# Down projection: weight sums in their own tile, made one item early; sevens and eights alternate; bank sums added by DMA

## The chip, the cores and the metric

The kernel runs on one core of a Trainium2 chip. A core has five engines, each with its own instruction queue that is worked through in order: TensorE (PE, matrix products), VectorE (DVE), ScalarE (ACT), GpSimd (POOL) and SyncE (SP, which here issues the loads of the weights). They meet only through semaphores. The metric is the time of one execution on the device in microseconds (us), as a median of runs. PE ran at its upper clock level, 2.4 GHz, all along: the granted clock of the profiled run is 0.996.

## What is computed

One layer on 256 tokens of width 2048. The change concerns its last sub-layer, a dense squared-ReLU MLP with a hidden width of 8192, and there the second product:

```python
x = x + rmsnorm(merged @ w_out[l], post_mix_g[l])
h = rmsnorm(x, pre_mlp_g[l])
f = jnp.square(jax.nn.relu(h @ w_up[l])) @ w_down[l]
x = x + rmsnorm(f, post_mlp_g[l])
```

Before it stands a token mixing part with four branches under sigmoid gates; one of its stages, the gate logits, uses the same product scheme as the down projection.

## The kernel before

**Weights.** Every product is made in three: weights and activations are split into a high and a low part, and PE computes high x high, high x low and low x high (L808 to L810 in `eight_sums`). The weights come in *items* of 1 MB, listed in program order by `w_items`. `w_emit` takes the next item, lets SP load it into one of three `raw` buffers, and cuts it into *pieces* of up to 128 x 1024. Of each piece `split` (L101 to L103) makes `hi` (ACT, a cast, L102) and `lo` (DVE, a subtraction, L103); both have four buffers. `w_get` keeps four pieces emitted ahead of the one PE works on. So a cast waits until PE is done with the piece four back, a load until the last reader of the item three back is done.

**Sums of weights.** The down projection works in groups. In a group `eight_sums` runs over eight items p, each with two weight blocks of 128 x 1024, and accumulates in eight PSUM banks (M1 to M8, four of tag `bank`, four of tag `aux`). An *eight* item is two pieces with four products each (24 matmuls). A *seven* item uses sums and differences of weight blocks and of activations (`sx`) and needs seven products instead of eight (21 matmuls) in four pieces: the first half of the item, a quarter of it, and two pieces of sums. The function `seven` makes these sums on DVE in the item's own `raw` buffer, the first behind the first piece's split (L161, 128 x 1024), the others behind the second's (L164, L165, 128 x 512):

```python
def first():
    V.tensor_tensor(b4[:, :, 0], b4[:, 1], b4[:, :, 0], ALU.subtract)
def second():
    V.tensor_tensor(b4[:, 1, 1], b4[:, 1, 1], b4[:, 0, 0], ALU.subtract)
    V.tensor_tensor(b4[:, 0, 1], b4[:, 0, 1], b4[:, 1, 1], ALU.subtract)
return [(b4[:, 0], first), (b4[:, 1, 1], second), (b4[:, :, 0], None), (b4[:, :, 1], None)]
```

`SEVEN` lists which p are sevens in the down stage, (1, 2, 4, 5); `SEVEN_G` does so for the gate stage, (1, 3, 5), where the same scheme runs six times.

**Stages.** The hidden width is worked in four quarters q. Each quarter has an up stage (`up`, blocks of 128 hidden columns, which also makes `sx` by `keep_sums`) and then two down groups h = 0, 1 one directly behind the other; the last quarter has one group, and then a plain product (`dn`) for the other half. `evac` (L1161 to L1166) moves a finished bank into `acc[h]`: in q = 0 by a copy on ACT (L1164), later by an add on DVE (L1166). `eight_sums` calls it one piece after the bank's last product (`late`, `settle`). `combine` (L1113) then adds the eight sums on DVE. The order on each engine is set by a scheduler from the program's dependencies; the rows of the change below show it.

Of the kernel before, what the change touches and what calls it, by code (L numbers as in the profile page):

```python
# [8 lines left out]
F32 = mybir.dt.float32  # L9
# [3 lines left out]
ALU = mybir.AluOpType  # L13
AX = mybir.AxisListType

P = 128
# [10 lines left out]
PC = 2048  # L27
CONSTS = P + 32 + 6 * 4 + 4 * CW
HC = 1024
# [3 lines left out]
QK_SCALE = 192 ** -0.5  # L33
TWO_PI = 6.283185307179586

SEVEN = (1, 2, 4, 5)
SEVEN_G = (1, 3, 5)


# [35 lines left out]
def trunk(ctx: ExitStack, tc: tile.TileContext, t: dict):  # L75
    nc = tc.nc
    V, A, G, T = nc.vector, nc.scalar, nc.gpsimd, nc.tensor

    cst = ctx.enter_context(tc.tile_pool(name="cst", bufs=1))
    wp = ctx.enter_context(tc.tile_pool(name="wp", bufs=1))  # L80
# [11 lines left out]
    def w2(name):  # L92
        return sm.tile([P, 512], F32, tag="w2", name=name, bufs=5)
# [56 lines left out]
    items = w_items()  # L150
    ready = []
    pending = []
    newest = []

    def seven(raw):


        b4 = raw.rearrange("p (a b n) -> p a b n", a=2, b=2)

        def first():  # L160
            V.tensor_tensor(b4[:, :, 0], b4[:, 1], b4[:, :, 0], ALU.subtract)  # L161

        def second():
            V.tensor_tensor(b4[:, 1, 1], b4[:, 1, 1], b4[:, 0, 0], ALU.subtract)  # L164
            V.tensor_tensor(b4[:, 0, 1], b4[:, 0, 1], b4[:, 1, 1], ALU.subtract)  # L165
        return [(b4[:, 0], first), (b4[:, 1, 1], second), (b4[:, :, 0], None), (b4[:, :, 1], None)]

    def w_emit():
        if not pending:
            it = next(items, None)  # L170
            if it is None:
                return False
            src, n, step = it
            raw = wp.tile([P, PC], F32, tag="raw", name="raw", bufs=3)
            if isinstance(step, str):
                nc.sync.dma_start(raw.rearrange("p (c n) -> p c n", c=2), src)
                pending.extend(seven(raw) if step == "seven" else [(raw[:, :HC], None), (raw[:, HC:], None)])
            else:
                nc.sync.dma_start(raw[:, :n], src)
                pending.extend((raw[:, o:min(n, o + step)], None) for o in range(0, n, step))  # L180
        src, then = pending.pop(0)
        hi = wp.tile([P, HC], F32R, tag="hi", name="hi", bufs=4)
        lo = wp.tile([P, HC], F32R, tag="lo", name="lo", bufs=4)
        if len(src.shape) == 3:
            parts = [a.rearrange("p (a n) -> p a n", a=2) for a in (hi, lo)]
        else:
            parts = [a[:, :src.shape[1]] for a in (hi, lo)]
        newest[:] = [e.ins for e in split(src, *parts)]
        if then:
            then()  # L190
        ready.append((hi, lo))
        return True

# [107 lines left out]
    for k in range(0, KD, 2):  # L301
        nc.sync.dma_start(xT[:, k:k + 2], t["xT"][:, k:k + 2])
        w = None
        for j in range(k, k + 2):
            if k < 4 or w is None:
                w, o = w_get(0), 0
# [237 lines left out]
    for b in range(4):  # L544
        ps = [bank("cva"), bank("cvg")]
# [174 lines left out]
    for b in range(4):  # L720
        ps = bank("su")
        block_tr(ps, hx)
        c = su[:, b * S:(b + 1) * S]
# [146 lines left out]
    for j in range(4):  # L870
        acc = None
        gts = [None] * 4
        for n, (xs, need, nk) in enumerate(order):
# [9 lines left out]
            elif n % 2 == 0:  # L883
                assert not tasks.live

                first = n + (n == 0)
# [26 lines left out]
            if n == 0:  # L913
                if j:
                    until(lambda: f"mx{j - 1}" in done)
                acc = t4n("acc")
# [44 lines left out]
    for c in range(4):  # L961
        ps = [bank(f"o{i}") for i in range(NT)]
        for k in range(0, KD if c < 3 else 8, 2):
            if c == 0 and k == 12:
# [3 lines left out]
                mp = ctx.enter_context(tc.tile_pool(name="mp", bufs=1))  # L968
# [109 lines left out]
    def keep_sums(p, ue, uo):  # L1078
        i = SEVEN.index(p)
        split(sums(ue, uo), sx[:, i, 0], sx[:, i, 1])  # L1080

    def first_hidden(fx):
# [17 lines left out]
            yield 1  # L1100
        done.add("u0")

    dr = ctx.enter_context(tc.tile_pool(name="dr", bufs=1, space=bass.MemoryType.DRAM))
    kept = dr.tile([P, NT, D], F32, name="kept")
    xr = mp.tile([P, NT, D], F32, tag="og", name="xr")
# [2 lines left out]
    acc = [None, None]  # L1108
# [29 lines left out]
    for q in range(NQ):  # L1138
        fx = big.tile([P, KQ, 2, S], F32R, tag="B", name="fx")
        if q == 0:  # L1140
            spawn(first_hidden(fx))
            spawn(second_norm())
        if q == NQ - 1:
            spawn(combine(1, lambda *a: None))
        ue = None
        for b in range(4 if q == 0 else 0, KQ):
            ps = bank("up")
            block_tr(ps, h2)
            u = w1("u")
            join(u, ps)  # L1150
            V.scalar_tensor_tensor(u, u, 0.0, u, ALU.max, ALU.mult)
            split(u, fx[:, b, 0], fx[:, b, 1])
            if b // 2 in SEVEN:
                if b % 2:
                    keep_sums(b // 2, ue, u)
                ue = u
        until(lambda: {"u0", "r2"} <= done)
        if q == 0:
            acc[0] = mp.tile([P, 8, 512], F32, tag="oo", name="acc0")
            acc[1] = mp.tile([P, 8, 512], F32, tag="og", name="acc1")  # L1160

        def evac(h, b, ps):
            if q == 0:
                A.copy(acc[h][:, b], ps[b])  # L1164
            else:
                V.tensor_tensor(acc[h][:, b], ps[b], acc[h][:, b], ALU.add)  # L1166

        for h in range(2 if q < NQ - 1 else 1):
            eight_sums(fx, lambda i, o: tuple(sx[:, i, a, o * P:(o + 1) * P] for a in range(2)), SEVEN,
                       lambda b, ps, h=h: evac(h, b, ps))  # L1170
        settle()
# [17 lines left out]
    ps = [bank(f"dn{i}") for i in range(NT)]  # L1189
# [8 lines left out]
    ps = [bank(f"dn{i}") for i in range(NT)]  # L1198
# [107 lines left out]
```

## Time and profile before

| | us |
|---|---|
| median of 3 runs (1500.91 to 1505.73) | 1502.41 |
| the profiled execution | 1501.62 |
| its span | 1499.9 |
| PE busy in it | 1472.8 |
| DVE busy | 1205.1 |
| ACT busy | 800.8 |
| POOL busy | 20.0 |

PE is busy 98% of the span, DVE 80%, ACT 53%, the DMA engines some 55%. A matmul's busy time in the trace is its whole way through the array, 0.39 us for 512 columns, while the next one starts after 0.227 us; a stretch is therefore read by its length and its count of matmuls. Idle time of PE is named with the event that ended it.

### The profile page before, as it was taken

Reading aid. Unit: us, or ns where it says so; the run is one execution under the profiler, and the core shown is the slowest. Engines: PE = TensorE matmul, PEld = TensorE weight load, DVE = VectorE, ACT = ScalarE, POOL = GpSimd, SP = SyncE. Lnnn points to the kernel's source line nnn. Section 1 sums busy time; section 2 is a strip of 40 time slices with the busy share of each in tenths; the row PEclk is TensorE's granted clock in tenths of the full one; section 3 lists DMA queues with packets and bytes.
Section 4 is the critical chain, followed back from the end, with each engine's and each line's share of the span. In section 5 each row is a group of like instructions: output and inputs, shape, how many; then the busy total and the mean of one; then the engine's idle time right before and its main releaser. Section 6 shows DMA issues by size and latency. Waiting matters only on the chain.

```text
span 1499.9 us, 18735 instructions
## 1 busy us (share of the span) xinstructions
PE 1472.8 (98%) x7192; PEld 1236.3 (82%) x7192; DVE 1205.1 (80%) x1697; ACT 800.8 (53%) x1078; POOL 20.0 (1%) x36
## 2 busy tenths in 40 slices
PE   9999999999999999999999999999999999999997
PEld 7988888888888888888878887888778887788875
DVE  6878788977798798796668888777997779987886
ACT  6655655445555555554445656655554545555552
POOL 0100000000000000000000000000000000000000
PEclk9999999999999999999999999999999999999999
DMA  8655544544655655656656645655556545655563
GB/s 268 219 192 173 180 171 153 187 172 167 226 200 172 226 203 170 226 203 241 245 213 253 216 164 200 213 194 194 169 171 227 194 166 199 210 184 196 168 253 113
DMA packets 57113, 295.76 MB, mean 197 GB/s; under 512 B 5120, under 2 KB 5248, under 8 KB 36544
## 3 DMA queue, kind: packets, MB, share of 16 engines
q1 hardware_dynamic: 55072, 280.68, 53.7%
q0 software_dynamic: 1952, 13.89, 2.6%
q8 instruction: 56, 0.92, 0.2%
q14 instruction: 33, 0.27, 0.1%
HBM read 290.36 MB, written 4.19 MB: 196 GB/s over the span
## 4 chain that ended last, share of the span: by engine, by line
PE 90%; DVE 5%; ACT 2%; issue 1%; DMA 1%; POOL 0%; POOLq 0%; ACTq 0%; SPq 0%; DVEq 0%
PE up L216 15%; PE sum L810 10%; PE sum L809 10%; PE sum L808 10%; PE up L219 8%; PE yb L205 2%; PE yb L206 2%; PE yb L207 2%; ACT hi L102 2%; DVE lo L103 2%; PE zg L205 2%; PE zg L207 2%; PE zg L206 2%; PE o L206 2%; PE o L205 2%; PE o L207 2%
## 5 line engine op out<-in xcount | busy, mean ns | idle before, releaser
L102 ACT CAST hi<-raw 128x1024 fp32r<-128x1024 f32 (+3 forms) x624 | 621.3, 1012 | 461.0 <-PE sum L810 112.3
L103 DVE TENSOR_TENSOR lo<-raw,hi 128x1024 fp32r<-128x1024 f32 (+3 forms) x624 | 720.9, 1173 | 168.3 <-ACT hi L102 160.8
L216 PE MATMUL up<-h,hi 128*128 128x512 f32 x960 | 229.9, 391 | 0.0
L216 PEld LDWEIGHTS up<-h,hi 128*128 128x128 f32 x960 | 176.3, 188 | 34.1
L808 PE MATMUL sum<-hi,fx 128*128 128x512 f32 x308 | 121.6, 395 | 12.3 <-ACT hi L102 12.3
L219 PEld LDWEIGHTS up<-h,lo 128*128 128x128 f32 x960 | 123.1, 191 | 4.7
L219 PE MATMUL up<-h,lo 128*128 128x256 f32 x960 | 124.8, 283 | 0.0
L809 PE MATMUL sum<-lo,hx 128*128 128x512 f32 x312 | 121.4, 389 | 0.0
L810 PE MATMUL sum<-hi,hx 128*128 128x512 f32 x312 | 121.4, 389 | 0.0
L808 PE MATMUL sum<-hi,hx 128*128 128x512 f32 x312 | 121.4, 389 | 0.0
L809 PE MATMUL sum<-lo,fx 128*128 128x512 f32 x308 | 120.0, 390 | 0.0
L810 PE MATMUL sum<-hi,fx 128*128 128x512 f32 x308 | 119.9, 389 | 0.0
L244 ACT COPY jn<-up 128x256 f32<-128x256 f32 x60 | 22.4, 372 | 115.3 <-PE up L216 115.3
L808 PEld LDWEIGHTS sum<-hi,fx 128*128 128x128 f32 x308 | 57.8, 188 | 30.3 <-ACT hi L102 18.4
L245 DVE TENSOR_TENSOR u<-up,jn 128x256 f32<-128x256 f32 x60 | 25.4, 424 | 65.0 <-ACT jn L244 65.0
L809 PEld LDWEIGHTS sum<-lo,hx 128*128 128x128 f32 x312 | 58.6, 188 | 12.3
L810 PEld LDWEIGHTS sum<-hi,hx 128*128 128x128 f32 x312 | 58.6, 188 | 12.2
L808 PEld LDWEIGHTS sum<-hi,hx 128*128 128x128 f32 x312 | 58.6, 188 | 12.2
L810 PEld LDWEIGHTS sum<-hi,fx 128*128 128x128 f32 x308 | 57.8, 188 | 12.3
L809 PEld LDWEIGHTS sum<-lo,fx 128*128 128x128 f32 x308 | 57.8, 188 | 12.2
L161 DVE TENSOR_TENSOR raw<-raw 128x1024 f32<-128x1024 f32 x46 | 56.0, 1218 | 0.2
L500 DVE SCALAR_TENSOR_TENSOR cy<-glu,consts,cy 128x253 f32<-128x253 f32 (+15 forms) x120 | 55.3, 463 | 0.6
(409 smaller groups left out, 2400.1 us busy)
## 6 DMA issues: line engine op xcount, KB each, us to landing
raw<-in_w_g SPq DMA_DIRECT2D x64, 1024.0 KB, 5.5
raw<-in_w_up SPq DMA_DIRECT2D x64, 1024.0 KB, 4.9
raw<-in_w_down SPq DMA_DIRECT2D x64, 1024.0 KB, 5.5
raw<-in_w_out SPq DMA_DIRECT2D x16, 1024.0 KB, 4.9
raw<-in_attn_proj SPq DMA_DIRECT2D x8, 1024.0 KB, 4.9
raw<-in_w_ca SPq DMA_DIRECT2D x4, 1024.0 KB, 4.9
raw<-in_w_cg SPq DMA_DIRECT2D x4, 1024.0 KB, 5.1
raw<-in_w_sv SPq DMA_DIRECT2D x4, 1024.0 KB, 4.8
```

The costliest lines, as they stand in the source:

```text
L102: a = A.copy(hi, src)
L103: return a, V.tensor_tensor(lo, src, hi.bitcast(F32), ALU.subtract)
L161: V.tensor_tensor(b4[:, :, 0], b4[:, 1], b4[:, :, 0], ALU.subtract)
L205: T.matmul(o, xh, wh, start=first, stop=False)
L206: T.matmul(o, xh, wl, start=False, stop=False)
L207: T.matmul(o, xl, wh, start=False, stop=last)
L216: T.matmul(ps, w[0][:, off:off + P], xs[:, k].rearrange("p a s -> p (a s)"), start=first, stop=last)
L219: T.matmul(ps[:, :S], w[1][:, off:off + P], xs[:, k, 0], start=False, stop=False)
L500: V.scalar_tensor_tensor(y, glu[:, b, :S - w], c, y, ALU.mult, ALU.add)
L808: T.matmul(ps[b], xh, wh, start=first, stop=False)
L809: T.matmul(ps[b], xh, wl, start=False, stop=False)
L810: T.matmul(ps[b], xl, wh, start=False, stop=not left[b])
```

## The change

The sums of a seven's weights go into a tile `comb` of their own (a free buffer of the tag `rg`) and not into `raw`. They are made during the item before: `w_emit` peeks at the next item, and if it is a seven it loads it at once and puts the first sum behind the split of the present item's second to last piece, the two others behind its last. `SEVEN` becomes (0, 2, 4, 6), so sevens and eights alternate. For q > 0 `evac` copies the bank on ACT into a tile `e` (tag `w2`, five buffers) and POOL adds `e` to `acc` by a DMA that accumulates. The gate stage comes before `comb` exists and keeps the sums in `raw`.

```diff
-SEVEN = (1, 2, 4, 5)
+SEVEN = (0, 2, 4, 6)
...
+    def load():
+
+        src, n, step = peeked.pop()
+        raw = wp.tile([P, PC], F32, tag="raw", name="raw", bufs=3)
...
+        nc.sync.dma_start(raw.rearrange("p (c n) -> p c n", c=2), src)
+        if step == "eight":
+            return [(raw[:, :HC], None), (raw[:, HC:], None)], []
...
+        t4 = comb[0].rearrange("p (b a n) -> p a b n", a=2, b=2) if comb else b4
+
+        def t13():
+            V.tensor_tensor(t4[:, :, 0], b4[:, 1], b4[:, :, 0], ALU.subtract)
+
+        def t2():
+            V.tensor_tensor(t4[:, 1, 1], b4[:, 1, 1], t4[:, 0, 0], ALU.subtract)
+
+        def t4_():
+            V.tensor_tensor(t4[:, 0, 1], b4[:, 0, 1], t4[:, 1, 1], ALU.subtract)
+        if comb:
+            return [(b4[:, 0], None), (b4[:, 1, 1], None), (t4[:, :, 0], None), (t4[:, :, 1], None)], [t13, t2, t4_]
...
+            pieces, before = coming.pop()
+            for f in before:
+                f()
+            pending.extend(pieces)
+            if comb and peek() and peek()[2] == "seven":
+                coming.append(load())
...
+        if coming:
+            before = coming[0][1]
+            for _ in range({0: 3, 1: 1}.get(len(pending), 0)):
+                if before:
+                    before.pop(0)()
...
+    comb.append(mp.tile([P, PC], F32, tag="rg", name="comb", bufs=2))
...
-                V.tensor_tensor(acc[h][:, b], ps[b], acc[h][:, b], ALU.add)
+                e = w2("e")
+                A.copy(e, ps[b])
+                G.dma_start(acc[h][:, b], e, accum_op=ALU.add)
```

Three places in the order of the engines. The first is DVE in the first down group of q = 1. Before, a seven stands right behind a seven (`raw_8858`, then `raw_8937`, then the eight `raw_8982`); L161, L164 and L165 are the three sums, L103 makes `lo`.

```order
L103 TENSOR_TENSOR lo_8927<-raw_8858,hi_8926 128x1024
L103 TENSOR_TENSOR lo_8940<-raw_8937,hi_8939 128x1024
L103 TENSOR_TENSOR lo_8948<-raw_8937,hi_8947 128x512
L161 TENSOR_TENSOR raw_8937<-raw_8937 128x2x512
L164 TENSOR_TENSOR raw_8937<-raw_8937 128x512
L165 TENSOR_TENSOR raw_8937<-raw_8937 128x512
L103 TENSOR_TENSOR lo_8962<-raw_8937,hi_8961 128x1024
L103 TENSOR_TENSOR lo_8973<-raw_8937,hi_8972 128x1024
L103 TENSOR_TENSOR lo_8985<-raw_8982,hi_8984 128x1024
L103 TENSOR_TENSOR lo_8992<-raw_8982,hi_8991 128x1024
```

After (the sums are now L181, L184, L187; `raw_9059` is an eight, `raw_9061` the seven behind it):

```order
L103 TENSOR_TENSOR lo_9034<-comb_6694,hi_9033 128x1024
L181 TENSOR_TENSOR comb_6694<-raw_9061 128x1024
L103 TENSOR_TENSOR lo_9050<-comb_6694,hi_9049 128x1024
L184 TENSOR_TENSOR comb_6694<-raw_9061,comb_6694 128x512
L103 TENSOR_TENSOR lo_9064<-raw_9059,hi_9063 128x1024
L103 TENSOR_TENSOR lo_9072<-raw_9059,hi_9071 128x1024
L187 TENSOR_TENSOR comb_6694<-raw_9061,comb_6694 128x512
L103 TENSOR_TENSOR lo_9084<-raw_9061,hi_9083 128x1024
L103 TENSOR_TENSOR lo_9094<-raw_9061,hi_9093 128x512
L103 TENSOR_TENSOR lo_9110<-comb_6694,hi_9109 128x1024
```

The first sum moved from behind its own item's two pieces to behind the third piece of the seven before, one item earlier; the two others stand behind pieces of that seven and of the eight between.

The second place is ACT where the second group of q = 1 follows the first. Before, it only casts (`raw_9120` is the last item of the first group, `raw_9151` the first of the second); the adds of the banks are on DVE.

```order
L102 CAST hi_9102<-raw_9100 128x1024 [waits DMAHW0_49,PE_49,Activation_49]
L102 CAST hi_9110<-raw_9100 128x1024 [waits PE_49,Activation_49]
L102 CAST hi_9122<-raw_9120 128x1024 [waits DMAHW1_49,DVE_49,PE_49]
L102 CAST hi_9134<-raw_9120 128x1024 [waits DVE_49,PE_49]
L102 CAST hi_9153<-raw_9151 128x1024 [waits DMAHW2_49,DVE_49,PE_49]
L102 CAST hi_9169<-raw_9151 128x1024 [waits DVE_49,PE_49]
L102 CAST hi_9187<-raw_9185 128x1024 [waits DMAHW3_49,DVE_49,PE_49]
L102 CAST hi_9206<-raw_9185 128x512 [waits DVE_49,PE_49]
L102 CAST hi_9228<-raw_9185 128x1024 [waits DVE_49,PE_49,Activation_49]
```

After, the copies of seven of the eight banks (`e`; M7, M5, M6, M2, M4, M3, M8 in this order) stand among the casts; `raw_9135` is the last item of the first group, `raw_9137` the first seven of the second. DMASW names a wait for a transfer that POOL issued.

```order
L102 CAST hi_9150<-raw_9135 128x1024 [waits DVE_49,PE_49]
L1196 COPY e_9172<-sum_8920 128x512 [waits PE_49]
L102 CAST hi_9162<-raw_9137 128x1024 [waits DMAHW2_49,DVE_49,PE_49]
L1196 COPY e_9175<-sum_8924 128x512
L102 CAST hi_9178<-raw_9137 128x512 [waits DVE_49,PE_49]
L1196 COPY e_9194<-sum_8936 128x512
L1196 COPY e_9213<-sum_8897 128x512 [waits PE_49]
L102 CAST hi_9197<-comb_6694 128x1024 [waits DVE_49,PE_49]
L1196 COPY e_9216<-sum_8932 128x512 [waits DMASW5_49]
L1196 COPY e_9231<-sum_8910 128x512 [waits DMASW6_49,PE_49,Activation_49]
L102 CAST hi_9219<-comb_6694 128x1024 [waits DVE_49,PE_49]
L1196 COPY e_9234<-sum_8966 128x512 [waits DMASW7_49,Activation_49]
```

The last three copies got a wait for a transfer of POOL's queue, and the casts of the second group's third and fourth piece stand behind such copies.

The third place is POOL at the end of the kernel. Before, `xr`, 2 MB, is its only transfer there.

```order
L1075 DMA kept<-xr 128x4096
L256 TENSOR_TENSOR r_7041<-r20p,mhalf 128x1
L256 TENSOR_TENSOR r_7171<-r21p,mhalf 128x1
L1179 DMA xr<-kept 128x4096
L256 TENSOR_TENSOR rf_12430<-rf0p,mhalf 128x1
L256 TENSOR_TENSOR rf_12473<-rf1p,mhalf 128x1
```

After:

```order
L1197 DMA acc_7418<-e 128x512 x8
L1197 DMA acc_7419<-e 128x512 x8
L1197 DMA acc_7418<-e 128x512 x2
L1210 DMA xr<-kept 128x4096
L1197 DMA acc_7418<-e 128x512 x6
L284 TENSOR_TENSOR rf_12511<-rf0p,mhalf 128x1
L284 TENSOR_TENSOR rf_12554<-rf1p,mhalf 128x1
```

Six of the last group's eight adding transfers stand behind `xr` in the queue.

## Rows read from the trace of the kernel before

**Rows 1.** The page's first part: busy us (share) x instructions of each engine.
```profile
PE 1472.8 (98%) x7192; PEld 1236.3 (82%) x7192; DVE 1205.1 (80%) x1697; ACT 800.8 (53%) x1078; POOL 20.0 (1%) x36
```

**Rows 2.** Busy time by stretch: four down stretches, `dn`, one gate group.
```profile
core 0: us, PE busy (x) PEld busy (x) DVE busy (x) ACT busy (x) POOL busy (x), PEclk, DMA share, GB/s
872.93:959.43 86.50, 83.70 (x361) 66.96 (x360) 72.44 (x75) 52.97 (x65) 0.00 (x0) 1.00 0.57 196
1048.50:1136.04 87.54, 83.75 (x361) 66.96 (x360) 80.41 (x90) 45.71 (x50) 0.00 (x0) 1.00 0.57 194
1225.11:1312.62 87.51, 83.71 (x361) 66.96 (x360) 80.62 (x91) 45.70 (x50) 0.00 (x0) 1.00 0.57 194
1401.69:1445.42 43.73, 41.84 (x181) 33.48 (x180) 38.89 (x45) 22.14 (x25) 0.58 (x1) 1.00 0.59 206
1445.42:1488.94 43.52, 43.52 (x193) 35.85 (x191) 31.14 (x44) 19.51 (x28) 1.00 (x1) 1.00 0.39 146
355.14:396.65 41.51, 41.51 (x184) 34.35 (x183) 37.54 (x42) 23.21 (x26) 0.00 (x0) 1.00 0.58 207
```

**Rows 3.** Waits of 872 to 1446: engine line <- releaser: us in total, times, longest.
```profile
PEld sum L808 <- ACT hi L102: 22.5, 28, 1.6
PE sum L808 <- ACT hi L102: 12.3, 14, 1.2
```

**Rows 4.** Timeline at two pairs: start, us, engine line op [idle before <- releaser].
```profile
882.80 1.22 DVE L161 TENSOR_TENSOR raw<-raw 128x1024 f32<-128x1024 f32 x1
884.05 0.69 DVE L164 TENSOR_TENSOR raw<-raw 128x512 f32<-128x512 f32 x1
884.13 1.05 ACT L102 CAST hi<-raw 128x1024 fp32r<-128x1024 f32 x1 [2.58 <-DVE raw L161]
884.78 0.69 DVE L165 TENSOR_TENSOR raw<-raw 128x512 f32<-128x512 f32 x1
...
885.59 2.00 ACT L102 CAST hi<-raw 128x1024 fp32r<-128x1024 f32 x2 [0.41 <-DVE raw L165]
886.68 0.19 PEld L808 LDWEIGHTS sum<-hi,fx 128*128 128x128 f32 x1 [1.15 <-ACT hi L102]
886.68 0.50 PE L808 MATMUL sum<-hi,fx 128*128 128x512 f32 x1 [0.71 <-ACT hi L102]
...
1078.93 0.50 PE L808 MATMUL sum<-hi,fx 128*128 128x512 f32 x1 [1.18 <-ACT hi L102]
```

**Rows 5.** Timeline: splits one behind the other on DVE, and the load behind.
```profile
879.70 3.18 DVE L103 TENSOR_TENSOR lo<-raw,hi 128x1024 fp32r<-128x1024 f32 x3 [1.48 <-ACT hi L102]
880.96 0.37 SPq L176 DMA_DIRECT2D raw<-in_w_down  x1
...
887.80 4.09 DVE L103 TENSOR_TENSOR lo<-raw,hi 128x1024 fp32r<-128x1024 f32 x4
888.94 2.95 DVE L103 TENSOR_TENSOR lo<-raw,hi 128x1024 fp32r<-128x1024 f32 x3
```

**Rows 6.** Issue to landing: L176's loads, its one of 872 to 882, three from 1435.6.
```profile
DMA to landing us min/median/max: 5.2/5.5/7.6
...
DMA to landing us min/median/max: 5.4/5.4/5.4
...
L179 SPq DMA_DIRECT2D raw<-in_w_down x3: 328/328/341, 1435.6 to 1442.5; - x3
...
DMA to landing us min/median/max: 9.5/10.5/11.5
```

**Rows 7.** Groups by line: adds (L1166) and copies (L1164): busy us, mean ns.
```profile
L1166 DVE TENSOR_TENSOR acc<-sum,acc 128x512 f32<-128x512 f32 x40 | 26.2, 682 | 0.0
L1164 ACT COPY acc<-sum 128x512 f32<-128x512 f32 x16 | 9.0, 588 | 1.3 <-PE sum L810 1.3
```

**Rows 8.** DMA issues of POOL's queue: count, KB each, median us to landing.
```profile
xr<-kept POOLq DMA_DIRECT2D x1, 2048.0 KB, 11.5
sgc<-in_sgu_b POOLq DMA_DIRECT2D x1, 256.0 KB, 4.5
sgg<-in_sgu_norm_g POOLq DMA_DIRECT2D x1, 256.0 KB, 3.6
```

More of the change, by code (lines that the diff above doesn't have):

```diff
@@ L153, in trunk @@
     newest = []
-    def seven(raw):
-        b4 = raw.rearrange("p (a b n) -> p a b n", a=2, b=2)
[L160 to L166, printed above, removed]
+    comb = []
@@ new lines, in trunk, with peek @@
+    peeked = []
+    coming = []
+    def peek():
+        if not peeked:
+            peeked.append(next(items, None))
+        return peeked[0]
+    def load():
+        src, n, step = peeked.pop()
+        raw = wp.tile([P, PC], F32, tag="raw", name="raw", bufs=3)
+        if not isinstance(step, str):
+            nc.sync.dma_start(raw[:, :n], src)
+            return [(raw[:, o:min(n, o + step)], None) for o in range(0, n, step)], []
+        nc.sync.dma_start(raw.rearrange("p (c n) -> p c n", c=2), src)
+        if step == "eight":
+            return [(raw[:, :HC], None), (raw[:, HC:], None)], []
+        b4 = raw.rearrange("p (a b n) -> p a b n", a=2, b=2)
+        t4 = comb[0].rearrange("p (b a n) -> p a b n", a=2, b=2) if comb else b4
[7 more added lines that the diff above has]
+            return [(b4[:, 0], None), (b4[:, 1, 1], None), (t4[:, :, 0], None), (t4[:, :, 1], None)], [t13, t2, t4_]
+        return [(b4[:, 0], t13), (b4[:, 1, 1], lambda: (t2(), t4_())), (t4[:, :, 0], None), (t4[:, :, 1], None)], []
@@ L168, in w_emit @@
     def w_emit():
         if not pending:
[L170 to L180, printed above, removed]
+            if not coming:
+                if peek() is None:
+                    return False
+                coming.append(load())
@@ L181, in w_emit @@
+            pieces, before = coming.pop()
[3 more added lines that the diff above has]
+            if comb and peek() and peek()[2] == "seven":
+                coming.append(load())
         src, then = pending.pop(0)
```

## The prediction

> **What bounds the kernel now.** I read four views in this order. The page's first part [rows 1] shows TensorE (PE) busy for 98% of the span, so a change can only win the time in which PE stands still, or lose by adding such time. The waits of PE [rows 3] then say where it stands still after 872 us: its one row is the product sum of the down projection waiting for ScalarE's (ACT's) cast `hi`, 14 times, 12.3 us; the weight-load row says the same. The busy table by stretch [rows 2] gives the exact price. The last down stretch (`dn`, no sums of weights) runs 192 matmuls in 43.52 us, 0.2267 us each, with PE busy all the time. The four stretches of down products hold 2, 2, 2 and 1 groups of 180 matmuls and last 86.50 + 87.54 + 87.51 + 43.73 = 305.28 us; 1260 x 0.2267 would be 285.60. **PE loses 19.7 us there.** One group of the gate stage, in the same table, does its 183 matmuls in 41.51 us, 0.2268 each: no loss, though it too has items of seven. Its sevens are items 1, 3, 5; in the down stage they are 1, 2 and 4, 5, in pairs.
>
> [Rows 4] show what a pair does. VectorE (DVE) makes the first sums of the second seven at 882.80 and the last at 884.78. ACT's cast of the piece that holds the first sums can only start at 884.13 (2.58 us idle, released by DVE), the next at 885.59, and PE, through with the two short pieces ahead, stops for 0.71 us, with the weight load 1.15 us late. Later pairs stop PE for 1.18 us. There are 14 pairs.
>
> **The change part by part.** I name the pieces of a seven s0 to s3 (6, 3, 6, 6 matmuls: 1.36, 0.68, 1.36, 1.36 us of PE) and those of an eight e0, e1 (12 each: 2.72 us). Seven and eight together are 45 matmuls, 10.20 us.
>
> *1. Alternation, sums ahead.* The number of matmuls, casts, subtractions and loads stays. After the change no seven follows a seven, and the sums for a seven are finished before its s0 is cast, so the wait of [rows 4] has no place left: **-19.7 us** if nothing comes late instead. The gate's 41.51 us group [rows 2] shows that alternating sevens alone already cost PE nothing.
>
> *2. What is late next: the load of a seven.* In the order of DVE (first excerpt of the change) the first sum of the next seven stands behind s2 of the present one, and it waits for that seven's load. The load's buffer is free only when `lo` of e1, one item back, is done. So there is a loop: first sum, lo s3, second sum, lo e0, lo e1, load, first sum of the seven after. Its price from rows: a 1024-wide operation is followed by the next after 1.14 us (888.94, 887.80 in [rows 5]), a dependent one after 1.25 (882.80 to 884.05 in [rows 4]), a 512 sum takes about 0.61 before an independent follower, and the last lo lasts 1.22. That is 1.14 + 1.25 + 0.61 + 1.14 + 1.22 = 5.36 us. The queue follows within 0.04 us (879.70 + 1.22 to 880.96 [rows 5]). An isolated load lands 5.4 us after its issue; all paired loads have 5.2 to 7.6, median 5.5 [rows 6]. With about 0.05 for the landing's signal the loop takes 10.85 us at 5.4, which is 0.65 more than PE's 10.20. PE does not feel that at once. Count from the moment at which PE ends e0: casts wait for the piece four back (`hi` has four buffers), lo e1 of that eight had ended at -2.6, the load lands at +2.8, so the first sum starts at about 2.9. PE needs lo of the next e0 at 7.7 (e1, s0 to s3, one matmul); it ends 4.2 us after the first sum's start (1.14 + 1.25 + 0.61 + 1.22). The sum may therefore start at 3.45. In a group alone the next such sum comes at 3.55: 0.1 us, nothing. In the three places where two groups follow each other directly the sums go on through the second group; the start grows four times in all (in one pair of the second group the second sum stands behind lo e1, which adds nothing): 2.9 + 4 x 0.65 = 5.5, or 2.0 us beyond the limit, 3 x 2.0 = **+6.0 us**. At 5.3 us a load this is about 3 x 1.5, at 5.9 about 3 x 5.0.
>
> *3. Adds by DMA.* 40 adds of 0.682 us leave DVE and 40 copies of 0.588 us come to ACT [rows 7]; both lie beside PE (in the 87.54 us stretch ACT is busy 45.7, and would be 55), so neither moves the end. What the 40 transfers add is waits. `e` has five buffers, so the sixth copy (M4) waits for the first transfer, M3 for M7's, M8 for M5's. The second excerpt shows who stands behind them on ACT: the casts of s2, s3 and the next e0. By the copies' places, M7's ends about 5.7 us and M5's about 5.8 us before the copy that reuses its buffer, and another 0.7 us is slack. A transfer under about 6.3 us is free at a seam. No row shows a transfer that adds; the nearest are the 256 KB loads of the same queue, 3.6 and 4.5 us [rows 8]; the far end is 11.5 us for 2 MB. I take 4 us: nothing.
>
> The Trainium skill, page Collectives: The Full Stack, section "The bandwidth ceiling: the fold count and why AG ≠ RS ≠ AR", says that an adding transfer costs two source reads, not an arithmetic delay; page DMA: Bandwidth & Descriptors, section "Anatomy of one DMA — SWDGE (gpsimd) path", gives 2.0 us plus bytes over 436e3. An estimate from the two for 512 KB read is 3.2 us, so the buffers would never bind and the sum would stay; a row of this kind is not in this trace.
>
> *4. They share the engines with loads.* Four of the eight transfers of a group fall into the load whose landing part 2 hangs on, at the two seams where both groups use DMA adds (the first seam copies straight into `acc`). How far a queue beside it delays a load is seen near the end: beside the 2 MB `xr` three loads took 9.5 to 11.5 us [rows 6], some 5 more. Four times 256 KB is half of that, at most 3; nothing if they slip into gaps (engines are 57% busy, [rows 2]). I take 1.5: 2 x 1.5 = **+3.0 us**, ends 0 and 6.
>
> *5. The end.* The third excerpt puts `xr` (2 MB, 11.5 us [rows 8]) ahead of six transfers in GpSimd's (POOL's) queue. `combine(0)` on DVE needs M2's; behind it stand lo of the later `dn` pieces, which are cast up to four pieces, 10.9 us, ahead. xr landing at about +9, then three transfers at 0.7 to 1.5 us, is +11 to +13.5 on the clock of part 2; the limit there is about +14. I take **+0.5**, ends 0 and 2. Loading `pog` earlier, `comb` in a free `rg` slot and the peeking cost no instruction on PE, DVE or ACT.
>
> **Sum.** -19.7 + 6.0 + 3.0 + 0.5 = -10.2 us. The profiled run took 1501.62 (span 1499.9), 0.8 less than the median 1502.41 of 1500.91 to 1505.73. So 1501.6 becomes 1491.4 and the median **1492**.
>
> **Rivals.**
> - *All hidden.* DVE gets further ahead than I count and the load never lands late: -19.7, about 1483. For it: the gate group without a loss. Against it: there the sums stand behind the seven's own casts, so no load is awaited that early.
> - *Given back.* Loads near 5.9 us (15), transfers that cost 3 at each seam (6) and 2 at the end: 23 of 19.7 us come back, 1498 to 1506, no difference. This is also where a change that only moves the stop to another piece ends. For it: second loads of close pairs in [rows 6] do reach 7.6.
> - *Slower.* The adding transfer itself is slow, and ACT stands at the `e` copies with all casts behind it. Above 6.3 us each further microsecond costs one at two seams; before the next up stage (two places) the slack is about 9.7, at the end about 8. The loss is 2(L - 6.3) + 2(L - 9.7) + (L - 8) = 5L - 40. With the 9.5 us of parts 2, 4 and 5 the change is slower than before by 4.5 us when this reaches 14.7, at L = 11; at L = 15 it is 35, and the time 1492 + 35 = 1527. For it: no row shows such a transfer. Against it: it would need three times the 3.6 to 4.5 us of [rows 8].
>
> **How the numbers follow.** A measurement of this kernel can tell about 0.3%, 4.5 us, from no change. Forecast (1486 to 1498): 0.50. All hidden (1480 to 1486): 0.25. Given back (1498 to 1507): 0.14. Slower: 0.11. Faster is the first two, 0.75; same 0.14; slower 0.11. The range goes from all hidden with the runs' own scatter, 1481, into the given-back case, 1501, which leaves about 2 in 10 out.
>
> **What would show it.** The 14 rows in which PE waits 0.7 to 1.2 us inside a pair must be gone, and the four down stretches must sum to about 295 us (285.6 if all is hidden). If part 2 is right, DVE's first sum into `comb` waits for the DMA of `raw`, longer from pair to pair, and PE stops at e0 pieces in the second group of a double stretch, none in the last single group. If part 3 is wrong, `e` copies on ACT wait for a DMA of `acc`. If part 4 is right, loads issued at the seam land in more than 6 us. A time above 1500 with the old stops gone would mean the DMA adds; above 1500 with stops inside s2, that the sums still come late.

## The result, and the profile after

The changed kernel takes **1513.7 us** (median of 4 runs, 1513.45 to 1516.83) where the kernel before, run beside it, takes 1502.88: ratio 1.0075, 95% interval 1.0054 to 1.0097. It is slower by 10.8 us. The prediction was 1492, range 1481 to 1501, so its sign was wrong. The profiled execution took 1513.6 with a span of 1511.9, 12.0 more than the span before.

The page's first part answers to [rows 1]: DVE gave away 28 us of work, ACT got 19, POOL 34, and PE is busy 98% again. That line doesn't show the loss.

```profile
PE 1480.3 (98%) x7192; PEld 1240.0 (82%) x7192; DVE 1176.7 (78%) x1657; ACT 819.8 (54%) x1118; POOL 54.0 (4%) x76
```

The busy table by stretch does; it answers to [rows 2]. A stretch runs from the first matmul of a stage to the first of the next; PEclk is the granted clock. Its rows are the down stretches of q = 0, 1, 2, the last up stage, the last down group and `dn`.

```profile
core 0: us, PE busy (x) PEld busy (x) DVE busy (x) ACT busy (x) POOL busy (x), PEclk, DMA share, GB/s
874.09:959.20 85.11, 84.01 (x362) 66.88 (x360) 69.60 (x72) 53.72 (x65) 0.00 (x0) 1.00 0.57 193
1048.27:1135.68 87.41, 84.14 (x362) 66.87 (x360) 69.61 (x72) 53.85 (x65) 11.85 (x14) 1.00 0.71 213
1224.74:1312.40 87.66, 84.19 (x362) 66.80 (x360) 69.61 (x72) 53.82 (x65) 11.78 (x14) 1.00 0.70 213
1312.40:1408.22 95.82, 91.87 (x514) 80.84 (x512) 68.83 (x109) 45.57 (x68) 1.84 (x3) 0.96 0.62 201
1408.22:1450.26 42.04, 41.74 (x182) 33.56 (x180) 34.16 (x36) 26.70 (x32) 5.52 (x7) 1.00 0.60 197
1450.26:1501.53 51.27, 46.19 (x193) 37.18 (x191) 29.50 (x42) 19.49 (x29) 2.82 (x4) 0.93 0.56 176
```

The four down stretches sum to 302.22 us, 3.06 less than before: of the 19.7 us to be won, 3 came. The last up stage took 89.07 before (1312.62 to 1401.69) and takes 95.82, 6.75 more. `dn`, up to the end of its last matmul, took 43.68 and takes 51.27, 7.59 more. The first down stretch starts 1.16 later and the end behind the last matmul is 0.43 shorter. I take the first of these for scatter: in the runs below that start lies between 873.4 and 875.7, whatever the kernel. Sum: -3.06 + 6.75 + 7.59 + 1.16 - 0.43 = +12.01.

The waits from 872 us on answer to [rows 3]. Columns: engine, line, what released it: us in total, times, longest.

```profile
DVE comb L181 <- DMA raw<-in_w_down: 33.5, 20, 3.4
...
ACT e L1196 <- DMA acc<-e: 20.6, 6, 9.9
DVE acc L1142 <- DMA acc<-e: 20.3, 2, 10.9
...
PEld sum L837 <- DVE lo L103: 19.9, 31, 2.2
...
PE sum L837 <- DVE lo L103: 8.0, 18, 1.8
...
PE up L247 <- DVE lo L103: 4.0, 1, 4.0
...
PE dn L234 <- DVE lo L103: 3.0, 1, 3.0
PE dn L233 <- ACT hi L102: 2.0, 1, 2.0
```

The 14 stops of PE at ACT's `hi` are gone. In their place PE waits for `lo`: 18 stops in the sums (31 of the weight load), one in `up` and one in `dn`, where one more at a cast `hi` stands before it. Behind them stand two kinds of wait: DVE's first sum L181 for the load of `raw`, 20 times, and ACT's copies and `combine`'s additions (L1142) for the adding transfers.

The timeline shows the two long ones. Rows: start, duration, engine, line, in brackets the idle time before and its releaser. First the last up stage, then `dn`:

```profile
1321.51 2.14 DVE L1142 TENSOR_TENSOR acc<-acc 128x512 f32<-128x512 f32 x3 [9.32 <-DMA acc<-e]
...
1324.84 2.08 PE L247 MATMUL up<-h,lo 128*128 128x256 f32 x8 [3.95 <-DVE lo L103]
...
1464.48 0.58 ACT L1196 COPY e<-sum 128x512 f32<-128x512 f32 x1 [9.88 <-DMA acc<-e]
...
1466.06 0.50 PE L233 MATMUL dn<-hi,fx 128*128 128x512 f32 x1 [2.04 <-ACT hi L102]
1466.99 1.42 DVE L1142 TENSOR_TENSOR acc<-acc 128x512 f32<-128x512 f32 x2 [10.94 <-DMA acc<-e]
...
1469.60 0.80 PE L234 MATMUL dn<-lo,fx 128*128 128x512 f32 x1 [3.03 <-DVE lo L103]
```

In `up`, `combine(1)` stands in DVE's queue for 9.32 us with the splits of the up pieces behind it; DVE's `lo` is what ends PE's stop. In `dn` both engines stand at once: ACT at the last `e` copy, DVE at `combine(0)`. The view of DMA issues (count, KB each, median us from issue to landing) answers to [rows 8]; behind it the least, median and greatest landing time of these 40:

```profile
acc<-e POOLq DMA_DIRECT2D x40, 256.0 KB, 10.1
```

```profile
DMA to landing us min/median/max: 3.2/10.1/19.1
```

The first adding transfers of the five groups land in 3.2 to 4.0 us; half of all 40 need more than 10. The eight ahead of the last up stage, one by one:

| issued | 1304.24 | 1306.62 | 1308.05 | 1309.48 | 1310.0 | 1311.70 | 1312.73 | 1316.66 |
|---|---|---|---|---|---|---|---|---|
| landed | 1307.4 | 1311.7 | 1315.7 | 1318.8 | 1321.5 | 1322.5 | 1323.7 | 1325.0 |

Five follow the first within 8 us of its issue, and they land up to 4.3 us apart. In this time they share the DMA engines with each other and with two loads of weights that SP issued at 1307.3 and 1310.0. The fifth is M2's, which `combine(1)` reads first; it starts at 1321.51.

### The profile page after: what moved, and what is told of

Its sections match the earlier page's. It is cut to its first block, busy times and chain, and to the rows that moved or that the text cites. A ratio compares the mean times of both kernels' runs of the same rounds, so it can differ in the third digit from the quotient of the medians.

```text
span 1511.9 us, 18849 instructions
## 1 busy us (share of the span) xinstructions
PE 1480.3 (98%) x7192; PEld 1240.0 (82%) x7192; DVE 1176.7 (78%) x1657; ACT 819.8 (54%) x1118; POOL 54.0 (4%) x76
## 4 chain that ended last, share of the span: by engine, by line
PE 64%; issue 23%; DMA 6%; DVE 3%; POOL 2%; ACT 0%; POOLq 0%; SPq 0%; DVEq 0%; ACTq 0%
PE up L244 7%; PE sum L837 6%; PE sum L838 6%; PE sum L836 6%; PE up L247 4%; DMA raw<-in_w_down 3%; PE yb L233 2%; PE yb L234 2%; PE yb L235 2%; DVE lo L103 2%; PE zg L235 2%; PE zg L233 2%; PE zg L234 2%; POOL acc L1197 2%; PE o L234 1%
## 5 line engine op out<-in xcount | busy, mean ns | idle before, releaser
L103 DVE TENSOR_TENSOR lo<-raw,hi 128x1024 fp32r<-128x1024 f32 (+2 forms) x568 | 653.6, 1168 | 148.7 <-ACT hi L102 144.2
L102 ACT CAST hi<-raw 128x1024 fp32r<-128x1024 f32 (+2 forms) x568 | 566.0, 1009 | 337.9 <-PE sum L838 81.8
L102 ACT CAST hi<-comb 128x1024 fp32r<-128x1024 f32 x56 | 58.8, 1051 | 93.7 <-PE sum L838 52.9
L103 DVE TENSOR_TENSOR lo<-comb,hi 128x1024 fp32r<-128x1024 f32 x56 | 68.5, 1222 | 20.1 <-ACT hi L102 19.5
L836 PEld LDWEIGHTS sum<-hi,hx 128*128 128x128 f32 x312 | 58.6, 188 | 12.3
## 6 DMA issues: line engine op xcount, KB each, us to landing
acc<-e POOLq DMA_DIRECT2D x40, 256.0 KB, 10.1
```

Of the source, the lines that this page charges most:

```text
L102: a = A.copy(hi, src)
L103: return a, V.tensor_tensor(lo, src, hi.bitcast(F32), ALU.subtract)
L836: T.matmul(ps[b], xh, wh, start=first, stop=False)
```

## The experiments

**Theory A**, formed from these rows: three separate losses. (1) The load loop costs 3.5 us in each double stretch and about 1.2 in the single one. (2) The adding transfers cost about 2.4 us at each of the two seams (where the second group of q = 1 and 2 follows the first), and (3) 6.75 and 7.6 us where `combine` reads `acc` soon after. **Theory B**: the sums made ahead are what loses, and the adds are harmless.

The result of every run first. Stretches are read as above, from the first matmul of one to that of the next, `dn` to the end of its last matmul; us. Times are medians; before beside e1 to e4 took 1502.86, beside the others 1502.65.

| | time | q0 | q1 | q2 | last up | q3 | dn |
|---|---|---|---|---|---|---|---|
| before | 1502.9 | 86.50 | 87.54 | 87.51 | 89.07 | 43.73 | 43.7 |
| after | 1513.7 | 85.11 | 87.41 | 87.66 | 95.82 | 42.04 | 51.3 |
| e1 after, DVE adds | 1492.9 | 85.81 | 84.23 | 84.00 | 89.06 | 42.54 | 43.7 |
| e2 before, DMA adds | 1513.4 | 86.54 | 87.20 | 86.52 | 93.13 | 43.27 | 51.3 |
| e3 before, alternating | 1486.4 | 81.81 | 82.72 | 82.70 | 89.07 | 40.90 | 43.7 |
| e4 after, sums later | 1500.6 | 81.81 | 83.62 | 83.62 | 95.95 | 40.90 | 52.5 |
| e5 e4, plain copies | 1488.2 | 81.82 | 81.82 | 81.82 | 89.32 | 40.90 | 46.6 |
| e6 e4, xr last | 1499.9 | 81.82 | 83.63 | 83.84 | 95.79 | 40.91 | 50.3 |
| e7 e4, DVE adds before last up | 1494.5 | 81.82 | 83.60 | 83.91 | 89.07 | 40.90 | 51.7 |
| e8 e4, GpSimd adds | 1501.9 | 81.81 | 88.97 | 88.94 | 95.03 | 40.94 | 43.8 |
| e9 e4, DVE adds | 1486.1 | 81.81 | 82.89 | 82.90 | 89.06 | 40.91 | 43.7 |
| e10 as e3 | 1485.5 | 81.81 | 82.70 | 82.73 | 89.07 | 40.90 | 43.7 |
| e11 e4, DMA adds at h = 0 only | 1486.8 | 81.82 | 83.69 | 83.65 | 89.07 | 40.91 | 43.7 |

### e1: the adds back on DVE

```diff
-                e = w2("e")
-                A.copy(e, ps[b])
-                G.dma_start(acc[h][:, b], e, accum_op=ALU.add)
+                V.tensor_tensor(acc[h][:, b], ps[b], acc[h][:, b], ALU.add)
```

> The changed kernel with one part undone: a bank is again added to acc on VectorE straight from PSUM, with no ScalarE copy and no adding transfer. Alternation and the sums made ahead stay. Theory A (three separate losses; between the profiles of before and after, the adds by DMA cost 6.75 us in the last up stage, 7.6 us in dn and about 2.4 us at each of two seams, 19.2 us together): the time falls from 1513.7 to about 1494.5, or up to 1500 if the eight adds of 0.68 us that return to VectorE at a seam push its loop back. Theory B (the adds are harmless, the sums made ahead are what loses): the time stays above 1510 and the up stage of the last quarter keeps its 95.8 us.

Measured: 1492.86 us, ratio to before 0.993 (0.9916 to 0.9945). The stretches of the profile, q = 1, the last up stage and `dn`:

```profile
1048.82:1133.05 84.23, 83.78 (x362) 66.87 (x360) 75.77 (x85) 46.83 (x50) 0.00 (x0) 1.00 0.57 194
1306.11:1395.17 89.06, 89.06 (x513) 78.72 (x512) 70.91 (x114) 45.03 (x66) 0.00 (x0) 1.00 0.56 195
1437.71:1481.39 43.68, 43.68 (x193) 35.85 (x191) 31.95 (x46) 18.89 (x27) 1.00 (x1) 1.00 0.41 159
```

Without the transfers the up stage and `dn` lose nothing, though DVE does more. Theory A holds, B falls. The time is 1.6 us under the 1494.5 of theory A. The adds by DMA cost 1513.7 - 1492.9 = 20.8 us here.

### e2: the DMA adds alone

```diff
-                V.tensor_tensor(acc[h][:, b], ps[b], acc[h][:, b], ALU.add)
+                e = w2("e")
+                A.copy(e, ps[b])
+                G.dma_start(acc[h][:, b], e, accum_op=ALU.add)
```

> The kernel before with only the third part done: copy on ScalarE and adding transfer in place of the VectorE add; pairs of sevens and sums in raw as before. Theory A: the losses of the adds do not need the rest of the change, so the last up stage is again about 6 to 7 us and dn 6 to 8 us longer than before, and the time is 1515 to 1522. Theory B: within 4 us of 1502.9, since nothing is loaded in a loop.

Measured: 1513.35 us, ratio 1.0073 (1.0056 to 1.009). This is 1.7 us under the range given, since the last up stage lost 4.06 instead of 6 to 7, and the seams nothing. `dn` lost 7.6 as in the changed kernel. The adds by DMA lose without the rest of the change.

### e3: the alternation alone

```diff
-SEVEN = (1, 2, 4, 5)
+SEVEN = (0, 2, 4, 6)
```

> The kernel before with only SEVEN = (0, 2, 4, 6): sums stay in raw, behind the seven's own two first pieces, adds stay on VectorE. If the stops belong to the pairs, as the gate group (41.51 us for 183 matmuls) says, the four down stretches fall from 305.3 to about 286 to 290 us and the time to 1483 to 1488. If a lone seven also stops PE at its first sum (VectorE has eight adds per group more here than in the gate group), half or more of the 19.7 us stays: 1493 to 1503.

Measured: 1486.36 us, ratio 0.9889 (0.9875 to 0.9904); 1485.50 in e10. The first, second and last down stretch:

```profile
873.95:955.76 81.81, 81.81 (x361) 67.59 (x360) 71.16 (x72) 53.79 (x65) 0.00 (x0) 1.00 0.61 208
1044.83:1127.55 82.72, 82.72 (x361) 67.19 (x360) 77.69 (x85) 46.79 (x50) 0.00 (x0) 1.00 0.61 205
...
1388.39:1429.29 40.90, 40.90 (x181) 33.79 (x180) 37.28 (x40) 24.07 (x26) 0.58 (x1) 1.00 0.61 214
```

One line of the change brings 17.15 of the 19.7 us (305.28 to 288.13). ACT still waits for the first sum, as in [rows 4], but PE has the two long pieces of an eight before it needs that cast, and no row of PE waiting is left in the down stretches.

### e4: the sums one item later

```diff
                 if before:
-                    before.pop(0)()
+                    with tc.issue_after(newest[1]):
+                        before.pop(0)()
```

This queues each sum on DVE behind the `lo` that the program lists ahead of it.

> The changed kernel with one order changed: the first sum is held behind lo of the eight's first piece e0, the other two behind lo of e1 or later, as the code lists them, in place of ahead of the seven's last piece. Everything else, the adds by DMA too, stays. Theory A (the first sum waits for the weights' load and passes the wait on to lo of e0; three double groups at 3.5 us and one single at 1.2 us, 11.7 us): VectorE no longer waits for a DMA of raw, the first down stretch, which has no adds, falls from 85.1 to about 82 us, and the time to about 1502. Rival (the stops at lo pieces come from VectorE's load as such): the stretch stays at 85 us and the time at 1513.

Measured: 1500.62 us, 13.1 less than the changed kernel; ratio to before 0.9986 (0.9977 to 0.9995). In the changed kernel, DVE's first sums in q = 0, where no add by DMA exists yet, stand like this:

```profile
885.12 1.23 DVE L181 TENSOR_TENSOR comb<-raw 128x1024 f32<-128x1024 f32 x1 [1.02 <-DMA raw<-in_w_down]
...
895.87 1.23 DVE L181 TENSOR_TENSOR comb<-raw 128x1024 f32<-128x1024 f32 x1 [1.34 <-DMA raw<-in_w_down]
...
900.15 0.50 PE L837 MATMUL sum<-lo,fx 128*128 128x512 f32 x1 [0.21 <-DVE lo L103]
...
907.08 1.23 DVE L181 TENSOR_TENSOR comb<-raw 128x1024 f32<-128x1024 f32 x1 [1.79 <-DMA raw<-in_w_down]
```

They are 10.75 and 11.21 us apart, where PE needs 10.20, and PE stops for `lo` in between. In e4 no row of DVE waiting for `raw` is left and the stretch is 81.81 us, without loss:

```profile
874.03:955.84 81.81, 81.81 (x361) 67.58 (x360) 69.94 (x72) 53.62 (x65) 0.00 (x0) 1.00 0.59 201
```

So the loop is real and cost 302.22 - 289.95 = 12.3 us in the four stretches. The losses of the last up stage and of `dn` stay (95.95 and 52.5 us): they don't depend on the loop. The next four kernels start from e4.

### e5: plain copies in place of the adds

```diff
-                G.dma_start(acc[h][:, b], e, accum_op=ALU.add)
+                G.dma_start(acc[h][:, b], e)
```

> The kernel of e4 (sums one item later, 1500.62 us) with the accumulation left out of the transfers: e is copied over acc, so the sum of the quarters is not computed; number, size and place of the transfers stay. If the adding itself is what makes them slow (in e4 they land 3.2 us after issue when alone, 9.4 in the median, one behind the other every 1 to 4 us), plain ones land in 3 to 5 us and the last up stage (95.95 us) and dn lose most of their 6.9 and 8.5 us: 1485 to 1490. If it is the queue beside the weights' loads, the landings stay near 9 and the time near 1500.

This leaves out the sum over the quarters. Measured: 1488.16 us. The landing times of the 40 transfers:

```profile
DMA to landing us min/median/max: 2.2/6.4/15.4
```

Time as the first case said, landings between the two. A plain copy takes 2.2 us alone and POOL 0.54 us to issue (0.85 with the add), and the seams lose nothing and the last up stage 0.25. So most of the loss is the adding itself. In `dn` 2.9 us stay: six copies land behind `xr`, up to 15.4 us after issue. That part comes with `xr` ahead of them in the queue.

### e6: xr behind the adds

```diff
-                G.dma_start(acc[h][:, b], e, accum_op=ALU.add)
+                added[:] = [G.dma_start(acc[h][:, b], e, accum_op=ALU.add)]
...
-    G.dma_start(xr, kept)
+    with tc.issue_after(added[0].ins):
+        G.dma_start(xr, kept)
```

`added[0]` is the last adding transfer.

> The kernel of e4 with one thing moved: the 2 MB load of xr is issued behind the last group's eight adding transfers, not ahead of six of them. Theory A (they wait for xr in their queue; in e4 six land 17 to 20 us after issue, behind the landing of xr at 1449.6): their landing comes 8 to 10 us earlier, the two stops of 3.2 and 3.0 us in dn shrink to 2 us or less together, and the time falls to 1492 to 1495; the last up stage keeps its 96 us. Rival (the adds are too slow even without xr, as ahead of the last up stage): dn still loses 5 us or more, 1497 to 1501.

Measured: 1499.92 us; the rival case. It is 0.7 less than e4, which ten runs of each don't tell from nothing (1497.6 to 1502.0 against 1497.8 to 1503.1). In the profiled runs the last group's transfers do land earlier (at most 11.4 us after issue), `dn` takes 50.28 instead of 52.54, and its two stops become one:

```profile
1447.98 2.14 DVE L1144 TENSOR_TENSOR acc<-acc 128x512 f32<-128x512 f32 x3 [9.29 <-DMA acc<-e]
...
1451.31 0.79 PE L235 MATMUL dn<-lo,fx 128*128 128x512 f32 x1 [3.75 <-DVE lo L103]
```

`combine(0)` waits 9.29 us, as long as `combine(1)` does ahead of the last up stage. By these two profiles `xr` was worth 2.3 us; the other 6.6 that `dn` loses come without `xr` ahead of the adds.

### e7: DVE adds ahead of the last up stage

```diff
+            elif (q, h) == (NQ - 2, 1):
+                V.tensor_tensor(acc[h][:, b], ps[b], acc[h][:, b], ALU.add)
             else:
                 e = w2("e")
```

> The kernel of e4, but the eight banks of the one group ahead of the last up stage (q = 2, h = 1) are added on VectorE as before the change; the other 32 adds stay DMA transfers. If the last up stage is long because the additions of combine(1) wait for these transfers on VectorE with the splits behind them, it falls from 95.95 to about 89.1 us and the time to about 1493.7; dn keeps its loss. If not, 1500.

Measured: 1494.52 us. The last up stage, and nothing else, is repaired:

```profile
1301.87:1390.94 89.07, 89.07 (x514) 78.73 (x512) 70.06 (x113) 45.27 (x66) 0.00 (x0) 1.00 0.56 195
```

### e8: the adds on GpSimd

```diff
-                G.dma_start(acc[h][:, b], e, accum_op=ALU.add)
+                G.tensor_tensor(acc[h][:, b], e, acc[h][:, b], ALU.add)
```

> The kernel of e4 with the 40 transfers replaced by 40 additions on GpSimd, from the same copy e; nothing goes through a DMA queue. No run so far has a GpSimd addition of 128x512. If one takes up to 2 us and disturbs nobody, all three losses go (about 1 us at each of two seams, 6.9 in the last up stage, 8.5 in dn): about 1484, at least not above 1487. If GpSimd slows VectorE's splits or takes 4 us and more, part stays: 1490 or above.

Measured: 1501.90 us, the second case. `dn` is repaired, but the stretches of q = 1 and 2 lose 7.1 us each against q = 0 and the last up stage 6.0. POOL and DVE at a seam:

```profile
1079.81 11.84 POOL L1198 TENSOR_TENSOR acc<-e,acc 128x512 f32<-128x512 f32 x6 [0.53 <-ACT e L1197]
...
1082.54 2.32 DVE L103 TENSOR_TENSOR lo<-raw,hi 128x1024 fp32r<-128x1024 f32 x1
1084.79 1.78 DVE L184 TENSOR_TENSOR comb<-raw,comb 128x512 f32<-128x512 f32 x1
1086.49 2.32 DVE L103 TENSOR_TENSOR lo<-raw,hi 128x1024 fp32r<-128x1024 f32 x1
```

A split that takes 1.22 us takes 2.32 beside a GpSimd addition, a 512-wide sum 1.78 instead of 0.69. Each is 1.1 us longer, whatever its own length. The additions themselves, least, median and greatest duration in ns:

```profile
L1198 POOL TENSOR_TENSOR acc<-e,acc x40: 1307/2272/2291, 1077.4 to 1454.7; 128x512 f32<-128x512 f32 x40
```

They too are longer than they need be: 1.31 us at best, 2.27 in the median.

### e9, e10, e11: what is left of the change

e9 is e4 with the DVE add of e1; e10 is e3 again; e11 is e9 with DMA adds where no `combine` follows:

```diff
+            elif h == 1 or q == NQ - 1:
+                V.tensor_tensor(acc[h][:, b], ps[b], acc[h][:, b], ALU.add)
             else:
                 e = w2("e")
```

> The kernel of e4 (sums one item later) with the adds on VectorE straight from PSUM, so alternation and comb without any DMA add. Against e1 (1492.86), which has the first sum ahead of the seven's last piece, it tells the load loop by itself: the stretch table of e1 gives 85.8 + 84.2 + 84.0 + 42.5 = 296.6 us for the four down stretches, and e4's first and last stretch (81.8, 40.9) say 288 or less: 1484 to 1486. If instead VectorE's adds at the seams push the later sums late, 1488 or more.

> The kernel of e3 (alternation alone) beside e9 on the same chip: what the tile comb and the sums made ahead add to the alternation. e3's down stretches are 81.8, 82.7, 82.7 and 40.9 us, 1.8 above twenty-eight items without a stop at the seams, so comb can bring at most about 2 us: 1486.4 again, and e9 between 1484.5 and 1486.5. If comb costs something of its own, e9 is the slower one.

> The kernel of e9, but the sixteen banks of the two groups that are followed by another group (h = 0, q = 1 and 2) are added by DMA; the 24 of the groups with combine behind them stay on VectorE. Here nobody reads acc soon, and only the buffers of e can make ScalarE wait. e4's stretches of 83.62 us against 81.81 say that each such seam still costs about 1.8 us where a VectorE add costs 0.9 (e3) or less: 1486 to 1488, at least not faster than e9. If the e copies relieve VectorE so that the seam is free, it is 1 to 2 us faster than e9.

Measured: 1486.10 (0.9891, 0.9876 to 0.9905), 1485.50 (0.9883, 0.9869 to 0.9898) and 1486.76 us (0.9897, 0.988 to 0.9913), the same time within the intervals. e9 against e1 isolates the loop without any DMA add: 288.5 against 296.6 us of down stretches, 8.1 us. e9 against e10: `comb` and the sums ahead, even with their loop removed, add nothing to the alternation. e11 against e9: a seam with DMA adds takes 0.8 us longer than one with DVE adds (83.69 and 83.65 against 82.89 and 82.90), so the transfers gain nothing in their most favourable place either. The best version is the kernel before with one line changed, 1486 us.

## Why the prediction was wrong, point by point

The forecast was -10.2 us and the span grew by 12.0, 22.2 more. Of these the last up stage and `dn` are 13.8 (6.75, and 7.59 where 0.5 was given): parts 3 and 5, the adds by DMA, turned the sign. Part 1 is 2.9 of it (288.5 us in e9 where 285.6 was forecast), part 2 is 2.1 (8.1, e1 against e9), part 4 is 2.6 (302.2 against 296.6 in e1, where 3.0 was forecast), the start and the end of the stretches 0.7.

**Part 1, alternation (-19.7): right in the main.** Alone it brings 17.2 us in the stretches, 16.5 in the time (e3). The prediction read from the gate group, with its sums in `raw`, that alternation alone costs PE nothing; it didn't go on to say that then the other two parts of the change have nothing left to win.

**Part 2, the load loop (+6.0): right in kind, too small.** The loop was put at 10.85 us; in q = 0 the second to sixth first sums are 10.75 to 11.28 apart, the last follows after 10.06. `lo` of e0 is late and the first sum waits for the load, as described. Its cost is 8.1 us without DMA adds and 12.3 with them. The stretch of q = 0 runs the same operations in the changed kernel and in e1 and took 85.11 and 85.81, so 0.7 us between two stretches with the loop in them say nothing. Two steps of the working failed. The group alone was put at no loss, but DVE waits for the load from the first group on (1.02 us at 885.12) and the single group of q = 3 lost 1.1. And a stop costs more than its idle row: in q = 0 the five rows of PE waiting sum to 1.1 us, the nine of the weight load to 4.5, and the stretch lost 3.3 against e4. The 14 old stops had shown the same: 12.3 us of rows, 19.7 lost. A smaller slip: at 5.9 us a load the prediction's own steps give 3 x 4.6, not 3 x 5.0.

**Part 3, adds by DMA (0): this is the step that failed**, in two ways. First the size. The transfer was put at 4 us from single loads of the queue, and the first of a group does take 3.2 to 4.0. But eight are issued within some 12 us beside the weights' loads, and the median is 10.1 us. A price for one was used where a price for eight in a row was needed. (At the two seams ACT waited only 0.5 and 0.4 us at the `e` copies: the limit of 6.3 us is about the first three transfers of a group, and these took 3.2 to 4.1.) Second the reader. The limits of 6.3, 9.7 and 8 us came from the five `e` buffers; that `combine(1)` on DVE reads `acc` right after the last group of q = 2, with the up pieces' splits behind it in the queue, was not listed. That alone is 6.75 us, and e7 takes it back. The prediction's own last sign, a time above 1500 with the old stops gone, pointed here.

The prediction's estimate of 3.2 us from the Trainium skill, from the page Collectives: The Full Stack, section "The bandwidth ceiling: the fold count and why AG ≠ RS ≠ AR", and the page DMA: Bandwidth & Descriptors, section "Anatomy of one DMA — SWDGE (gpsimd) path", agrees with the 3.2 us of an isolated transfer in this trace. It led to the same error, since it too is a price for one. By the same working an estimate for the plain copy is 2.6 us; e5 measured 2.2. That an add is two source reads, as the first of them says, fits the rows of the DMA queues below, where an add holds the engines twice as long as a plain copy.

**Part 4, sharing at the seams (+3.0): right in kind, too small.** Seams with DMA adds cost 3.2 and 3.7 us more than with DVE adds in the changed kernel (against e1), and 0.7 each without the loop (e4 against e9). The load that the loop waits for at a seam landed after 7.1 and 7.3 us, 1.7 and 1.9 over an isolated one, near the 1.5 taken; but the next one was late too (6.3 and 6.4 us), and the sum had one load per seam.

**Part 5, the end (+0.5): wrong by 7 us.** The six transfers were to pass behind `xr` at 0.7 to 1.5 us each, once it had landed at about +9. On that clock, whose zero is here 1450.26 - 2.72 = 1447.5, `xr` took 15.3 us, not 11.5, and landed at 1460.6, which is +13; M2's transfer was issued at 1447.9 and took 19.1, which is +19.5 instead of +11 to +13.5, past the limit of +14. Behind `xr` the first add needed 3.8 us and the others 1.3 each: of the three prices only the last was right. And with `xr` out of the way (e6) the adds are still too late; `xr` is some 2.3 us of the loss.

**The rivals.** "Slower" named the right mechanism, a slow transfer, with a condition (11 us) that the median nearly meets, but with the `e` buffers alone as the place. ACT did stand there (6 times, 20.6 us), and in `dn` one of the two stops, 2.04 us, came from it; the stops of 3.95 and 3.03 us came from `combine`. The reason against it, three times the price of a single load, was wrong. By its formula 5L - 40 an L of 10.1 gives 10.5 us, against 15.8 for `up`, `dn` and the two seams without a loop (6.75 + 7.59 + 1.5). It got 0.11. *Given back* put loop and seams at 21 us, where they took 13.7 (302.2 against 288.5), and the end at 2.

**What the clock adds.** The stop is 3.95 of the 6.75 us that the last up stage lost. Stretches of 5 us of the changed kernel, four from the stop in `up` on and three from `dn` (the clock is the number after POOL):

```profile
1320.00:1325.00 5.00, 1.05 (x9) 0.84 (x7) 3.42 (x5) 1.02 (x1) 0.00 (x0) 0.85 0.76 136
1325.00:1330.00 5.00, 5.00 (x16) 4.32 (x17) 5.00 (x8) 0.41 (x1) 0.00 (x0) 0.50 0.64 210
1330.00:1335.00 5.00, 5.00 (x30) 4.38 (x30) 4.93 (x11) 2.68 (x4) 0.00 (x0) 0.96 0.56 210
1335.00:1340.00 5.00, 5.00 (x31) 4.49 (x30) 4.28 (x8) 3.10 (x5) 0.00 (x0) 1.00 0.61 210
...
1465.00:1470.00 5.00, 0.90 (x2) 0.59 (x3) 2.98 (x4) 2.76 (x5) 0.84 (x1) 0.69 0.83 151
1470.00:1475.00 5.00, 5.00 (x15) 3.92 (x15) 5.00 (x8) 2.98 (x6) 0.00 (x0) 0.63 0.62 211
1475.00:1480.00 5.00, 5.00 (x23) 4.12 (x23) 5.00 (x7) 3.39 (x6) 0.00 (x0) 1.00 0.64 210
```

After the stop of 3.95 us PE is busy all the time but starts 16 matmuls in 5 us instead of 31: the granted clock is 0.50, the lower level (1.2 GHz). 15 matmuls at 5/31 us are 2.4 us on top of the stop. After `dn`'s two stops it is 15 instead of the 23 of a 5 us stretch of `dn` at the upper level, another 1.7. No part of the prediction had this.

**What the DMA queues add.** Packets, MB and share of the time of the 16 DMA engines; q0 is POOL's queue, q1 SP's. First the changed kernel from 1308 to 1324, while the adds ahead of the last up stage move; then the 4 us from 1319 on, in which no load is beside them; then 1 us of e5 (1304 to 1305) in which plain copies move alone. A share over 100% says that times of packets overlap.

```profile
q0 software_dynamic: 1003, 1.83, 65.5%
q1 hardware_dynamic: 288, 2.10, 37.4%
...
q0 software_dynamic: 441, 0.81, 111.7%
...
q0 software_dynamic: 129, 0.42, 103.8%
```

For 16 us the two queues together take 103%: the engines are full, with seven adds and two loads. Alone the adds move 0.81 MB in 4 us, which is 256 KB in 1.3 us, the same 1.3 us at which they land behind `xr`. Plain copies move 0.42 MB in 1 us, twice as much. So eight adds need some 10 us of all 16 engines (an estimate, 8 x 1.3), and the loads of weights come on top. By these rows a landing after 10 us is a wait for full engines; the prediction had a time to landing where it needed a share of the engines.

**Still open:** how the engines divide their time between the two queues, and so why a single gap reaches 4.3 us. No run was made that changes the loads beside the adds.

## What to carry to other kernels

Price a queue by what is issued into it together and by what shares its engines, not by one of its transfers, and list every reader of what it writes, on each engine, with what stands behind that reader. Test the parts of a bundled change apart: one line of this one won 16.5 us, and the rest gave back 27. Operations taken off an engine that isn't the bound bought nothing here, whoever took them.

## What the runs showed of the hardware

An adding transfer of 256 KB lands in 3.2 us alone, a plain one in 2.2; eight within some 12 us, beside weight loads, land after 8.8 to 10.9 us in the median of a group (the four ahead of `xr`), plain ones after 5.9 to 6.6 (e5). With nothing beside them adds move 0.20 MB in a microsecond, plain copies 0.42.

GpSimd and DVE slow each other when both work on two tensors in SBUF (e8): DVE's operations take 1.1 us longer each, GpSimd's additions 1.0. The Trainium skill, page SBUF — State Buffer, section "SBUF: two separate sides", says that the two share a pair of ports which one holds for a whole instruction while the other stands still. By that rule each operation waits out one of the other side; the rows agree, since the operation behind a split of 1024 starts 2.25 us after it (1082.54 to 1084.79) instead of 1.14 [rows 5], and the short sums are longer by the same 1.1 us.

After a stop of PE of 3.95 us the granted clock was 0.50, the lower level, in the next 5 us, with 16 matmuls instead of 31, and 1.00 from 5 us later on; the stops of 0.7 to 1.2 us before the change left the clock at 1.00 [rows 2, 4].
